# RG-LRU gate products as two 64-row matmuls on the halves of TensorE's array

## The chip, the cores and the metric

The kernel runs on one core of a Trainium2 chip. The metric is device time in microseconds of one execution. The engines are TensorE (PE, with its weight loads PEld), VectorE (DVE), ScalarE (ACT), GpSimd (POOL, nearly unused here) and SyncE (SP, which issues the transfers). One execution was profiled; the spans and rows below are from it.

## The reference, cut to what matters

One residual block of a streaming encoder on 512 tokens of width 1024: a Mamba-2 branch and an RG-LRU branch side by side, a gated merge of both, and a convolutional feed-forward part. The RG-LRU branch is what the change touches:

```python
gate = gelu(u_y)
xc = causal_dwconv(u_x, conv_w, conv_b)                  # 4 taps
xb = xc.reshape(b, s, 16, 64)                            # 16 blocks of 64 channels
r = sigmoid(einsum("bshi,hij->bshj", xb, wr) + br)       # each block has its own 64 x 64
i = sigmoid(einsum("bshi,hij->bshj", xb, wi) + bi)
log_a = -8 * r * softplus(-lam)
a = exp(log_a)
bx = sqrt(-expm1(2 * log_a)) * i * xc
h = associative_scan(a, bx)                              # h_t = a_t h_(t-1) + bx_t
y_b = h * gate
```

All of it is float32.

## The kernel before

Activations lie channel-major: 128 channels on the partitions, 512 tokens along the columns. Every float32 operand of a product is split in two (a high part in the fast matmul format, and the rest), and each product is three matmuls, high by high, high by low and low by high, that add up in one PSUM bank (`mm3`).

The weights come as 149 slabs of 128 x 1024. SyncE loads a slab (`raw`), ScalarE writes its high part (`whi`, L50 as all calls that keep their order) and VectorE its low part (`wlo`, L180). A slab is split two products ahead (`AHEAD = 2`). A product against the 1024-deep activations is 24 matmuls.

The order of TensorE's and of ScalarE's instructions is that of the code. VectorE's is put together by the compiler's planner from the code's order and its own costs. Work that follows a product is registered with `after(n, ...)` and written n slabs later, in `tick`; `step` holds back pieces of the Mamba-2 branch that fill VectorE between products.

The RG-LRU part runs over eight tiles of 128 channels, each with two of the 64-channel blocks. Tile i has its product, its convolution (`conv`, L225), two slabs later the split of `xc` and of the gate weights `wg` (`lru_split`, L611 and L612), and three slabs after its own product the gate products and what follows (`lru_gates`). So the gate group of tile i stands on TensorE behind the product of tile i + 2, and on ScalarE behind the first convolution step (`tmp<-ps,pcs`) of that product. The gate weights of a tile are two 128 x 128 matrices, one for r and one for i, each with two 64 x 64 blocks on its diagonal and zeros elsewhere. Each is one `mm3` and one tanh (sigmoid by tanh) with a bias per channel.

ScalarE then does an exp, a tanh (both `L<-tmp,nsp`) and a square; VectorE a multiplication with `xc` (L629) and one for the root (L632). After every fourth tile come a square root of 2048 columns on ScalarE, a multiplication of 2048 columns (L636) and four scans (L642) on VectorE. The buffers named `L` are four; two sets of three are needed, so the second set waits for the scans of the first.

Behind that the eight products of the gelu branch follow: `lru_out` multiplies gelu (ScalarE) by the scan's result (L660) and splits it (`Y`, L197); the merge needs all eight.

Of the kernel before, what the change touches and what calls it, by code (L numbers as in the profile page):

```python
# [8 lines left out]
F32 = mybir.dt.float32  # L9
# [5 lines left out]
P = 128  # L15
D = 1024          # model width = SSM inner = LRU width
S = 512           # tokens
KT = D // P       # contraction tiles of a 1024-deep product
TT = S // P       # token tiles, also the SSD chunks
HEADS = 16  # L20
HD = 64
# [4 lines left out]

# columns of the per-channel parameter array
C_SCW, C_SCB = 0, 48
# [5 lines left out]
N_PC = 356  # L34
# columns of the row parameter array
R_POST, R_POST2, R_HEAD = 0, D, 2 * D
# [3 lines left out]
class InOrder:  # L40
    """An engine whose instructions keep the order in which they are written here."""

# [11 lines left out]
def block_kernel(ctx: ExitStack, tc, x, slabs, wgate, pc, rows, out):  # L54
# [37 lines left out]

# [1 line left out]
    xts = []  # L94
# [10 lines left out]

# [1 line left out]
    pending, steps = [], []  # L107
# [5 lines left out]
    def step(cost, fn, *args):  # L113
        """A step for the vector engine, of that many microseconds."""
        steps.append((cost, fn, args))

    def next_slab():
        """What follows needs the tensor engine to have gone on, or another engine's result."""
        steps.append(None)
# [19 lines left out]

# [1 line left out]
    n_slabs = slabs.shape[0]  # L141
# [57 lines left out]
    def split_scaled(hi, lo, src, w):  # L199
        """Split of src * w, w one value per partition."""  # L200
        A.mul(hi, src, w)
        V.scalar_tensor_tensor(out=lo, in0=src, scalar=w, in1=hi.bitcast(F32),
                               op0=ALU.mult, op1=ALU.subtract)
# [7 lines left out]
    def product(acts):  # L211
        """One 128-column slab against [1024, 512] activations: [128 columns, 512 tokens]."""
        w = slab()
        acc = ps()
        accumulate(acc, w, acts)
        return acc

    def conv(acc, w0, bias, taps):
        """Causal depthwise convolution along the tokens."""
        t = tmp()  # L220
        A.activation(t, acc, AF.Identity, bias=pcs[:, bias:bias + 1],
                     scale=pcs[:, w0 + taps - 1:w0 + taps])
        for d in range(1, taps):
            w = w0 + taps - 1 - d
            V.scalar_tensor_tensor(out=t[:, d:], in0=acc[:, :S - d], scalar=pcs[:, w:w + 1],  # L225
                                   in1=t[:, d:], op0=ALU.mult, op1=ALU.add)
        low_parts()
        return t
# [6 lines left out]
    def use_sqrt():  # L235
        """Has the scalar engine ready for square roots."""
        A.activation(tiny.tile([P, 1], F32, tag="ready", name="ready"), EPS1, AF.Sqrt)

    def sumsq(src, s=None, junk=None):
        """Sums of squares along the columns."""  # L240
        if s is None:
            s = tiny.tile([P, 1], F32, tag="ssq", name="ssq", bufs=16)
        if junk is None:
            junk = work.tile([P, S], F32, tag="junk", name="junk", bufs=1)
        A.activation(junk, src, AF.Square, accum_out=s)  # L245
        return s

    def inv_rms(parts, width, e):
        """(sum of parts / width + e) ** -0.5, as two factors; one part may be [128, n]."""
        n = parts[0].shape[1]  # L250

        def t(name):
            return tiny.tile([P, n], F32, tag=f"{name}{n}", name=name, bufs=4 if n == 1 else 1)

        for s in parts[:-1]:
            b = t("mean")
            A.activation(b, s, AF.Identity, scale=1.0 / width, bias=e)
            e = b
        r = t("root")
        A.activation(r, parts[-1], AF.Sqrt, scale=1.0 / width, bias=e)  # L260
        v = t("var")
        V.tensor_scalar(out=v, in0=parts[-1], scalar1=1.0 / width, scalar2=e,
                        op0=ALU.mult, op1=ALU.add)
        V.reciprocal(r, r)
        q = t("step")
        if n == 1:
            V.scalar_tensor_tensor(out=q, in0=r, scalar=v, in1=r, op0=ALU.mult, op1=ALU.mult)
        else:
            V.tensor_mul(q, r, r)
            V.tensor_mul(q, q, v)  # L270
        V.tensor_scalar(out=q, in0=q, scalar1=-0.5, scalar2=1.5, op0=ALU.mult, op1=ALU.add)
        return r, q
# [3 lines left out]

# [1 line left out]
    use_sqrt()  # L278
# [17 lines left out]

# [1 line left out]
    def causal(value, name):  # L298
        m = const.tile([P, P], F32, name=name)      # value where column >= row
        G.memset(m, value)  # L300
        G.affine_select(out=m, in_=m, compare_op=ALU.is_ge, fill=0.0, base=0,
                        pattern=[[1, P]], channel_multiplier=-1)
        return m
# [4 lines left out]
    G.memset(ones, 1.0)  # L308
    halfb = const.tile([P, 32], F32, name="halfb")  # halves of br, bi, gate_b
    V.tensor_scalar_mul(halfb, pcs[:, C_BR:C_BR + 32], 0.5)  # L310
    nsp4 = const.tile([P, 8], F32, name="nsp4")     # -4 softplus(-lambda)
    nega = const.tile([P, HEADS], F32, name="nega")

    def softplus(u, e):
        """max(u, 0) + log1p(e) with e = exp(-|u|), the logarithm by its atanh series."""
        n = u.shape[1]
# [15 lines left out]

# [1 line left out]
    def ssd_input(j, dst=None):  # L334
# [96 lines left out]
    for g in range(2):  # L431
        ssd_input(10 + g, Cc[:, g, :])
        tick()
# [1 line left out]
    xs = big.tile([P, TT, D], F32, tag="C", name="xs", bufs=2)  # L435
# [57 lines left out]
    def carry(c, g):  # L493
        """What earlier chunks bring to this one, and the state after it."""
        h0 = c * HEADS + 8 * g
# [69 lines left out]

# [1 line left out]
    for j in range(2):  # L567
# [16 lines left out]

# [1 line left out]
    for c in range(2):  # L586
# [19 lines left out]
    xcs = big16("Y", F32R).rearrange("p (i two) s -> p i two s", two=2)  # L606
    wgs = big16("Y", F32R).rearrange("p i (two w c) -> p i two w c", two=2, w=2)

# [5 lines left out]
    def lru_gates(i, xc):  # L614
# [3 lines left out]
        aa, uu, qq = grp["t"]  # L618
        gates = []
        for w in range(2):  # L620
            rp = ps()
            mm3(rp, wgs[:, i, 0, w], wgs[:, i, 1, w], xcs[:, i % 4, 0], xcs[:, i % 4, 1], True, True)
            s = tmp()
            A.activation(s, rp, AF.Tanh, bias=halfb[:, 8 * w + i:8 * w + i + 1], scale=0.5)
            gates.append(s)
        sp = nsp4[:, i:i + 1]
# [18 lines left out]
    for i in range(KT):  # L645
        wg = tiny.tile([P, 2, P], F32, tag="wg", name="wg", bufs=2)
        tc.keep_in_program_order(nc.sync.dma_start(out=wg, in_=wgate[i]))
# [19 lines left out]

# [1 line left out]
    m1 = []  # L669
# [23 lines left out]

# [1 line left out]
    def row_tile(r0):  # L695
# [4 lines left out]
    def norm_add(acts, n_slab, e, row, res, tail, lead, target, done):  # L700
        """target = res + RMSNorm(acts @ W) * row; token tile by token tile over the last slabs."""
        first = work.tile([P, TT, S], F32, tag="M", name="first", bufs=1)
# [114 lines left out]

# [1 line left out]
    early = []  # L819
# [51 lines left out]
def _layout(x, mix_pre_norm, mix_post_norm, w_in, ssm_conv_w, ssm_conv_b, ssm_dt_bias, ssm_a_log,  # L871
# [5 lines left out]
    def cols(w):  # L877
        """[1024, 128 n]: slab j holds [row in tile, row tile, column] of its 128 columns."""
        n = w.shape[1] // P
        return w.reshape(KT, P, n, P).transpose(2, 1, 0, 3).reshape(n, P, D)  # L880

    def rws(w):
        """[K, 1024]: per column half, slabs of two 128-row tiles by 512 columns."""
        n = w.shape[0] // (2 * P)
# [8 lines left out]
    up = cols(np.asarray(w_ffn_up)[0])  # L893
    dts = np.zeros((1, P, KT, 8, HEADS), np.float32)     # the dt columns twice, then zeros
    dts[0, :, :, :2] = dtw.reshape(KT, P, 1, HEADS).transpose(1, 0, 2, 3)
# [8 lines left out]
    ])  # L904
    wgate = np.zeros((8, P, 2, P), np.float32)
    for n, g in enumerate((lru_wr, lru_wi)):
        g = np.asarray(g)[0].reshape(8, 2, HD, HD)
        for e in range(2):
            s = slice(e * HD, (e + 1) * HD)
            wgate[:, s, n, s] = g[:, e]  # L910

    def chan(v, n):
        """[taps, 128 n] to [128, n, taps]."""
        v = np.asarray(v)[0].reshape(-1, n, P)
# [27 lines left out]
```

## Time and profile before

| what | value |
|---|---|
| three runs | 887.65, 887.66, 889.61 us; median 887.66 us |
| profiled execution, first to last instruction | 885.8 us |
| granted TensorE clock, mean | 0.999 |
| TensorE busy | 872.5 us (98%), 4050 matmuls |
| TensorE weight loads | 724.0 us (82%) |
| VectorE busy | 519.9 us (59%) |
| ScalarE busy | 392.8 us (44%) |

The time of an execution lies some 1.9 us over the span from its first to its last instruction. Matmuls are pipelined: the duration shown for one is longer than the distance to the next. Line numbers are those of the kernel before; L50 is the helper that records TensorE's and ScalarE's calls in order, so these are told apart by their tiles.

### The profile page before, as it was taken

How to read it: one execution, taken by the hardware profiler on the slowest of the kernel's cores; microseconds unless marked ns; L12 is line 12 of the kernel's file. 1: busy time of each engine (PE TensorE's matmuls, PEld its weight loads, DVE VectorE, ACT ScalarE, POOL GpSimd, SP SyncE). 2: the span in 40 equal slices, each digit the busy share in tenths (PEclk: the TensorE clock that was granted, in tenths of full speed). 3: DMA queues.
4: the chain of work that ended last, by engine and by line, in shares of the span. 5: the costliest groups of instructions: out<-in, count | busy, mean ns of one | idle time of the engine just before them, and what ended most of it. 6: DMA issues, size and time to landing. Idle time of an engine off the chain costs nothing.

```text
span 885.8 us, 10176 instructions
## 1 busy us (share of the span) xinstructions
PE 872.5 (98%) x4050; PEld 724.0 (82%) x4050; DVE 519.9 (59%) x732; ACT 392.8 (44%) x602; POOL 1.7 (0%) x14
## 2 busy tenths in 40 slices
PE   7999999999999999999999999999999999999996
PEld 6888887888878888888888988888888888888885
DVE  6777657987874554344467566666666666223225
ACT  6454535579584334222355444444444444213222
POOL 0000000000000000000000000000000000000000
PEclk9999999999999999999999999999999999999999
DMA  6332232222325332222370022222222222322212
GB/s 224 102 137 95 95 118 84 92 87 72 142 96 182 128 119 72 96 95 95 102 252 27 25 94 96 95 95 96 95 95 95 95 95 95 117 98 95 95 48 96
DMA packets 26192, 91.61 MB, mean 103 GB/s; under 512 B 3040, under 2 KB 4256, under 8 KB 25632
## 3 DMA queue, kind: packets, MB, share of 16 engines
q1 hardware_dynamic: 26144, 90.95, 30.1%
q8 instruction: 32, 0.52, 0.2%
q14 instruction: 16, 0.13, 0.0%
HBM read 88.81 MB, written 2.13 MB: 103 GB/s over the span
## 4 chain that ended last, share of the span: by engine, by line
PE 88%; DVE 5%; ACT 5%; issue 1%; DMA 1%; SPq 0%; DVEq 0%; ACTq 0%
PE ps L50 88%; ACT L L50 1%; DVE L L642 1%; DMA raw<-slabs 1%; DVE wlo L180 1%; ACT whi L50 1%; ACT tmp L50 1%; DVE tmp L660 0%; DVE L L636 0%; ACT L50 0%; ACT junk L245 0%; ACT M L50 0%; DVE Y L197 0%; ACT Y L50 0%; ACT junk L50 0%
## 5 line engine op out<-in xcount | busy, mean ns | idle before, releaser
L180 DVE TENSOR_TENSOR wlo<-raw,whi 128x1024 fp32r<-128x1024 f32 x139 | 169.7, 1222 | 140.5 <-ACT whi L50 137.9
L50 PE MATMUL ps<-C,whi 128*128 128x512 f32 x768 | 241.6, 389 | 0.0
L50 PE MATMUL ps<-H,whi 128*128 128x512 f32 x720 | 224.1, 394 | 1.5 <-DVE H L50 1.5
L50 ACT CAST whi<-raw 128x1024 fp32r<-128x1024 f32 x137 | 143.0, 1045 | 110.9 <-PE ps L50 105.6
L50 PEld LDWEIGHTS ps<-C,whi 128*128 128x128 f32 x768 | 144.1, 188 | 29.9
L225 DVE SCALAR_TENSOR_TENSOR tmp<-ps,pcs,tmp 128x511 f32<-128x511 f32 (+1 forms) x156 | 116.6, 748 | 80.4 <-ACT tmp L50 77.9
L50 PE MATMUL ps<-C,wlo 128*128 128x512 f32 x416 | 161.8, 389 | 0.0
L50 PEld LDWEIGHTS ps<-H,whi 128*128 128x128 f32 x720 | 134.1, 188 | 31.1 <-issue 2.4
L50 PE MATMUL ps<-H,wlo 128*128 128x512 f32 x352 | 137.5, 391 | 0.4 <-DVE wlo L180 0.3
L50 ACT ACTIVATE tmp<-ps,pcs 128x512 f32<-128x512 f32 x68 | 53.1, 780 | 128.2 <-PE ps L50 128.2
L50 PEld LDWEIGHTS ps<-C,wlo 128*128 128x128 f32 x416 | 78.1, 188 | 16.1
L50 PE MATMUL ps<-whi,H 128*128 128x512 f32 x256 | 81.4, 394 | 0.0
L50 PEld LDWEIGHTS ps<-H,wlo 128*128 128x128 f32 x352 | 66.1, 188 | 15.2 <-DVE wlo L180 1.2
L50 PE MATMUL ps<-whi,Y 128*128 128x512 f32 x192 | 59.6, 389 | 0.0
L50 PEld LDWEIGHTS ps<-whi,H 128*128 128x128 f32 x256 | 48.1, 188 | 10.3 <-issue 0.5
L50 PE MATMUL ps<-wlo,H 128*128 128x512 f32 x128 | 49.9, 389 | 0.0
L50 ACT CAST Y<-tmp 128x512 fp32r<-128x512 f32 x24 | 14.9, 621 | 66.9 <-DVE tmp L690 36.8
L50 ACT ACTIVATE tmp<-ps,halfb 128x512 f32<-128x512 f32 x32 | 21.5, 687 | 49.6 <-PE ps L50 49.6
L50 PEld LDWEIGHTS ps<-whi,Y 128*128 128x128 f32 x192 | 36.0, 188 | 7.5
L50 PE MATMUL ps<-Y,whi 128*128 128x512 f32 x128 | 40.5, 396 | 0.2 <-DVE Y L197 0.2
L50 PE MATMUL ps<-whi,L 128*128 128x512 f32 x128 | 39.7, 389 | 0.0
L50 PE MATMUL ps<-wlo,Y 128*128 128x512 f32 x96 | 37.3, 389 | 0.0
(167 smaller groups left out, 848.1 us busy)
## 6 DMA issues: line engine op xcount, KB each, us to landing
raw<-slabs SPq DMA_DIRECT2D x149, 512.0 KB, 3.2
quad<-x SPq DMA_DIRECT2D x8, 512.0 KB, 4.3
M<-acsD SPq DMA_DIRECT2D x4, 1024.0 KB, 4.6
out<-tmp SPq DMA_DIRECT2D x8, 256.0 KB, 2.1
wg<-wgate SPq DMA_DIRECT2D x8, 128.0 KB, 3.3
quad<-rows SPq DMA_DIRECT2D x2, 512.0 KB, 4.7
pcs<-pc SPq DMA_DIRECT2D x1, 178.0 KB, 7.1
acsD<-acsT SPq DMA_DIRECT2D x1, 32.0 KB, 2.9
```

What stands on the lines that cost most here:

```text
L50: return lambda *args, **kw: self.tc.keep_in_program_order(op(*args, **kw))
L180: V.tensor_sub(*late.pop(0))
L225: V.scalar_tensor_tensor(out=t[:, d:], in0=acc[:, :S - d], scalar=pcs[:, w:w + 1], in1=t[:, d:], op0=ALU.mult, op1=ALU.add)
L642: V.tensor_tensor_scan(out=qq[:, e, :], data0=aa[:, e, :], data1=uu[:, e, :], initial=0.0, op0=ALU.mult, op1=ALU.add)
```

## The change

The zero blocks go. The gate weights of a tile become one 128 x 128 array: its upper 64 rows hold the r and i columns of the first block side by side, its lower 64 rows the i and r columns of the second. `wg` is loaded and split with half the columns. In place of two times three matmuls of 128 rows there are three pairs of 64-row matmuls; one of a pair works on the upper 64 partitions and the other on the lower, each into a PSUM bank of its own, `rps[0]` and `rps[1]`. Each bank then holds r in one half of its partitions and i in the other. The two tanh of 128 partitions become four of 64 partitions, all of 512 columns, two of which read one half of the partitions and write the other. Both banks and both `tmp` buffers are taken at the group's start. Comments were dropped from the file too.

```diff
-    wgs = big16("Y", F32R).rearrange("p i (two w c) -> p i two w c", two=2, w=2)
+    wgs = big16("Y", F32R).rearrange("p i (two w c) -> p i two w c", two=2, w=2)[:, :, :, 0, :]
...
-        gates = []
+        halves = slice(0, HD), slice(HD, P)
+        rps = ps(), ps()
+        for n, (u, v) in enumerate(((0, 0), (0, 1), (1, 0))):
+            for b in range(2):
+                mm(rps[b], wgs[halves[b], i, u], xcs[halves[b], i % 4, v], n == 0, n == 2)
+        gates = [tmp(), tmp()]
         for w in range(2):
-            rp = ps()
-            mm3(rp, wgs[:, i, 0, w], wgs[:, i, 1, w], xcs[:, i % 4, 0], xcs[:, i % 4, 1], True, True)
-            s = tmp()
-            A.activation(s, rp, AF.Tanh, bias=halfb[:, 8 * w + i:8 * w + i + 1], scale=0.5)
-            gates.append(s)
+            for b in range(2):
+                A.activation(gates[w][halves[b], :], rps[b][halves[w ^ b], :], AF.Tanh,
+                             bias=halfb[halves[b], 8 * w + i:8 * w + i + 1], scale=0.5)
...
-        wg = tiny.tile([P, 2, P], F32, tag="wg", name="wg", bufs=2)
+        wg = tiny.tile([P, P], F32, tag="wg", name="wg", bufs=2)
...
-    wgate = np.zeros((8, P, 2, P), np.float32)
-    for n, g in enumerate((lru_wr, lru_wi)):
-        g = np.asarray(g)[0].reshape(8, 2, HD, HD)
-        for e in range(2):
-            s = slice(e * HD, (e + 1) * HD)
-            wgate[:, s, n, s] = g[:, e]
+    wr, wi = (np.asarray(g)[0].reshape(8, 2, HD, HD) for g in (lru_wr, lru_wi))
+    wgate = np.concatenate([np.concatenate([wr[:, 0], wi[:, 0]], 2),
+                            np.concatenate([wi[:, 1], wr[:, 1]], 2)], 1)
```

## Rows read from the trace of the kernel before

**Rows 1.** The page, busy time of each engine, share of the span.

```profile
PE 872.5 (98%) x4050; PEld 724.0 (82%) x4050; DVE 519.9 (59%) x732; ACT 392.8 (44%) x602; POOL 1.7 (0%) x14
```

**Rows 2.** Stretches: length, PE, PEld, DVE, ACT, POOL busy us; clock, DMA share, GB/s.

```profile
155.00:184.00 29.00, 29.00 (x138) 24.28 (x137) 26.28 (x45) 18.00 (x25) 0.00 (x0) 1.00 0.29 94
...
200.00:220.00 20.00, 20.00 (x89) 16.48 (x89) 15.02 (x22) 19.63 (x25) 0.00 (x0) 1.00 0.25 79
220.00:232.00 12.00, 11.63 (x60) 9.35 (x59) 12.00 (x16) 4.50 (x7) 0.00 (x0) 1.00 0.36 133
...
260.00:880.00 620.00, 618.90 (x2878) 516.76 (x2878) 321.75 (x433) 240.03 (x368) 0.00 (x0) 1.00 0.29 100
```

**Rows 3.** The chain that ended last, 130 to 270 us: start us, us, what.

```profile
129.78 54.36 PE ps L50 x240
...
184.16 0.69 ACT tmp L50
...
190.18 1.65 DVE L L636
...
196.70 3.38 DVE L L642 x3
...
200.09 0.82 ACT L L50
...
218.03 2.29 DVE L L636
...
259.90 10.18 PE ps L50 x48
```

**Rows 4.** Waits from 155 to 260 us: in total, times, longest.

```profile
ACT L L50 <- DVE L L642: 5.1, 1, 5.1
...
PEld ps L50 <- DVE wlo L180: 1.2, 2, 0.8
```

**Rows 5.** TensorE's timeline, the gate group of tile 3: start us, us.

```profile
182.60 1.52 PE L50 MATMUL ps<-Y 128*128 128x512 f32 x6
```

**Rows 6.** Timeline around the 32-row transposes, matmuls (PE) and weight loads (PEld).

```profile
29.64 0.39 PE L50 MATMUL ps<-H,wlo 128*128 128x512 f32 x1
29.96 0.43 PE L50 MATMUL ps<-ident,tmp 32*128 32x32 f32 x4
30.32 0.72 PE L50 MATMUL ps<-H,whi 128*128 128x512 f32 x2
...
30.32 0.30 PEld L50 LDWEIGHTS ps<-H,whi 128*128 128x128 f32 x2
```

**Rows 7.** ScalarE's timeline, tanh and exp of tiles 3 and 5.

```profile
183.48 1.37 ACT L50 ACTIVATE tmp<-ps,halfb 128x512 f32<-128x512 f32 x2
184.75 1.51 ACT L50 ACTIVATE L<-tmp,nsp 128x512 f32<-128x512 f32 x2
...
203.09 1.25 ACT L50 ACTIVATE tmp<-ps,halfb 128x512 f32<-128x512 f32 x2
204.23 1.52 ACT L50 ACTIVATE L<-tmp,nsp 128x512 f32<-128x512 f32 x2
```

**Rows 8.** VectorE's timeline at 24 us, a copy of 32 lanes.

```profile
24.62 0.68 DVE L360 COPY tmp<-ps 32x512 f32<-32x512 f32 x1 [0.49 <-PE ps L50]
```

**Rows 9.** The tile `wg`: duration ns min/median/max, first and last start us.

```profile
L612 DVE TENSOR_TENSOR Y<-wg,Y x8: 414/419/426, 147.1 to 202.3; 128x256 fp32r<-128x256 f32 x8
```

**Rows 10.** VectorE's timeline, 208 to 225 us.

```profile
208.55 0.69 DVE L629 SCALAR_TENSOR_TENSOR L<-tmp 128x512 f32<-128x512 f32 x1
209.16 0.69 DVE L612 TENSOR_TENSOR Y<-tmp,Y 128x512 fp32r<-128x512 f32 x1
...
223.68 1.22 DVE L180 TENSOR_TENSOR wlo<-raw,whi 128x1024 fp32r<-128x1024 f32 x1
```

**Rows 11.** TensorE at tile 7's gate group, and its weight load at 225 us.

```profile
209.80 1.56 PE L50 MATMUL ps<-Y 128*128 128x512 f32 x6
...
224.95 0.19 PEld L50 LDWEIGHTS ps<-H,wlo 128*128 128x128 f32 x1 [0.45 <-DVE wlo L180]
```

## The prediction

> **What bounds the kernel now.** I began with the busy shares of the page: TensorE is busy for 98% of the span [rows 1]. That says that most of the time is a row of matmuls with hardly a gap, but not that every matmul taken out gives its time back. So the second view is the table of stretches around the change [rows 2]. From 260 us on TensorE waits for next to nothing. In 200 to 220 us, where the last gate products lie, ScalarE is busy 19.63 of 20 us, and in 220 to 232 us VectorE is busy all 12 us. Two other engines are full just there. The third view is the chain that ended last [rows 3]: one unbroken piece of TensorE up to 184.13 us, then ScalarE and VectorE alone until 259.90 us, then TensorE again. The reader is to see that for 76 us the end is set by the recurrence work that follows the gate products, while TensorE keeps itself busy from weights split in advance. The fourth view says how much TensorE has to spare there [rows 4]: its weight loads do wait for `wlo`, the low halves of the weights, though only 1.2 us in all. Its reserve is used up. Whatever makes the chain between 184 and 260 us later makes TensorE later by as much; whatever makes TensorE faster inside it turns into waiting.
>
> **TensorE's part.** One group of gate products is six matmuls in 1.52 us, the last of them 0.39 [rows 5]: they start 0.227 us apart, 1.36 us a group, 10.9 us for eight. Their number does not change. With two 64-row matmuls at a time in the two halves of the array, six take three slots, 0.68 us. Nothing in the trace runs two at a time, so concurrency itself is unseen; what can be checked is the weight load: two loads of 128 columns in a row take 0.30 us, one of them 0.19, so they lie 0.11 us apart [rows 6], so two fit a slot of 0.227 us. The change of shape is seen once, around the four 32-row transposes [rows 6]: the first starts 0.32 us after the full matmul ahead of it instead of 0.227, and behind them the first full matmul holds its successor off by 0.33 us (0.72 less the 0.39 of one). That is 0.1 us at each end; the last transpose ends some 0.08 us before the full matmul starts. I take 0.28 us for in and out. So one group is 0.68 + 0.28 = 0.96 us and gives 0.40 us, eight give 3.2 us. Bounds for the gain g of a group: 0.49 us if the 0.08 us is the transposes' own, 0.30 us if the second half starts a load (0.11 us) late; and -0.28 us if the halves run one after the other.
>
> The Trainium skill speaks of the same place: "TensorEngine Tiling (Array Packing)", Overview, gives a theoretical speedup of up to 2x for a dimension of 64, and its Tiling Modes says that changing the mode drains the engine. By the 2x alone g would be 0.68 us and the sum below +2.4 us; by the row with the change of shape it is +3.2 us. I go by the row; the trace agrees with the drain, 0.1 us at each end. The same page's PSUM Bottleneck says that tiling does not speed up the emptying of PSUM, which is here the tanh on ScalarE; 19.63 busy us of 20 [rows 2] bear that out for the stage behind tile 4.
>
> **ScalarE's part.** The two tanh (`tmp<-ps,halfb`, 128x512) become four of 64x512. The engine now needs 1.27 us from the first tanh of group 3 to the exp behind it (183.48 to 184.75), because the second half of the products comes 0.68 us after the first; where both are there in time it is 1.14 us (203.09 to 204.23), 0.57 us each [rows 7]. What half the lanes cost is not in the trace on this engine. The nearest row is VectorE's: a copy of 32 lanes by 512 columns takes 0.68 us [rows 8], an operation of 128 lanes by 512 columns 0.69 [rows 10]. The tanh keep their columns and lose only lanes, so I take 0.57 us for each half, 2.28 us for four; the lower bound is half of that, 0.29 us, with which four cost what two cost now. The extra is 2.28 - 1.27 = +1.0 us for group 3 and 2.28 - 1.14 = +1.14 us for those that run packed.
>
> The Trainium skill's "ScalarE: Activation LUTs", What ACT_TABLE_LOAD costs, counts one element per cycle in each lane, by which idle lanes save nothing and the sum is the +3.2 us below; no run here shows it for this engine.
>
> **The rest of the change.** VectorE splits 128 columns of `wg` in place of 256: the longer of its two operations is 0.42 us now [rows 9]. Halving the columns is worth at most 0.21 us for it and as much for the other. They end by 203 us and none lies on the chain, since in the part of it that is VectorE's the rows are others [rows 3]; so I count nothing; if one did lie on it, that would be a gain of at most 0.4 us. The eight loads of `wg` halve, and nothing on the chain waits for one. Both PSUM tiles are taken at once instead of in turn; two were in use before too. The arithmetic on the sums is the same. Costed at nothing, together.
>
> **The sum along the chain.** Each group k is worked off on ScalarE behind the convolution of the product ahead of it, so it moves with TensorE.
> 1. Where the chain leaves TensorE (group 3, 182.60 us), groups 0 to 2 have given 3 x 0.40: -1.2 us. ScalarE keeps up there: 18.0 us busy in the 29 us up to 184 [rows 2] with the work of three groups; with 1.0 more for each it is 21 in some 28.
> 2. Group 3's tanh: +1.0. The square root, the 2048-column multiplication and the four scans [rows 3] begin 0.2 us earlier.
> 3. Group 4's tanh lie ahead of the 5.05 us in which ScalarE waits for the scans to free a buffer [rows 4]: its 1.14 us vanish there.
> 4. Groups 5, 6 and 7 run on ScalarE without a pause up to the second square root: 3 x 1.14 = +3.4 us. At 218.03 us the chain is at -1.2 + 1.0 + 3.4 = +3.2 us.
> 5. From there VectorE is full to 232 us, and the `wlo` for which TensorE waits at 224.95 us [rows 10, 11] comes 3.2 us later, and so does TensorE. The rest of the chain and everything behind 259.90 us move along.
>
> TensorE meanwhile comes 3.2 us too early, so its waits grow by 6.4 us: some 2 us at the product behind group 6; up to 3 us at group 7, since the split of its input ends at 209.85 us, 0.05 us behind the group's start, and stands on VectorE behind the multiplication of 208.55 us that needs group 6's tanh [rows 10, 11]; and some 2 us at 225 us. The profiled execution has a span of 885.8 us; the median of the runs is 887.66, so 1.9 us lie around the span. I forecast 887.7 + 3.2 = **890.9 us**, slower by 0.36%. With g from 0.30 to 0.49 the sum is +3.5 to +2.9: 890.6 to 891.2, and with half a microsecond for the order on VectorE 890.3 to 891.6.
>
> **Rivals.**
> *The halves don't overlap.* For it: the trace has no pair that runs together. Against it: nothing but different rows, different banks and loads that fit. Then g is -0.28: +0.8 + 1.0 + 3.4 = +5.3 us, 893.0.
>
> *VectorE's order changes, and it is not slower.* VectorE's instructions are put in order by a planner, which will see other lengths. The multiplication of 190.18 us takes 2.29 us, as its twin at 218.03, and ends at 192.4; three scans take 3.38 us, so four directly behind it would end at 196.9 us in place of 200.0 [rows 3], and what VectorE does between them now, convolution and a weight split, would come later. ScalarE then goes on 3.1 us earlier, and the sum is +0.1, 887.8 us. It decides from a lead of 0.5 us on (3.2 less 2.7). For it: ScalarE's 5.05 us of waiting [rows 4] are just that order. Against it: the convolution was planned ahead of the scans, and no input of either changes places.
>
> *Half a tanh costs half.* With 0.29 us each, steps 2 and 4 fall away: -1.2 us, 886.5 us, since the chain still starts behind only three faster groups. Against it stands the copy of 32 lanes.
>
> *The gain arrives.* Cheap halves and scans first together would leave TensorE as the bound: -3.2 us, and at best the 1.2 us of waits that it has now [rows 4]: 883.3 to 884.5 us.
>
> *The clock.* The granted clock is 1.00 in each of the stretches [rows 2], and no wait there is longer than half a microsecond. Waits of 2 to 3 us close together are not in this stage of the trace. If the clock fell to the lower of its two levels behind one, half a product (12 slots of 0.227 us) would cost 2.7 us more: 893.6 us.
>
> **How the numbers follow.** A measurement of this kernel can tell about 0.3%, 2.7 us, from no change. Chances: the forecast 0.48; no overlap 0.13; clock 0.05; VectorE's order, wholly or in part (887.8 to 890.3), 0.21; cheap halves 0.05; the gain arrives 0.08. Slower by over 0.3%: 0.48 but for a small part, 0.13 and 0.05, so 0.63; within: 0.29; faster: 0.08. The range leaves out the gain that arrives and the far end of the worst cases: 886.4 to 893.6 us.
>
> **What the profile after would show.** Right: a group of gate products in about 1 us, with pairs that start together; four tanh in 2.3 us; ScalarE without a pause from about 200 to 221 us; TensorE waiting some 6 us in all between 200 and 235 us for `wlo` and for the input of group 7; nothing new behind 263 us. Wrong: groups of 1.6 us (no overlap); tanh of 0.3 us; scans that end before 198 us; granted clock under 1.00. A TensorE that reaches the last stage earlier than now would refute the reading that the chain, not TensorE, sets this stage.

## The result, and the profile after

Slower, and by twice the forecast: 7.1 us where 3.2 were forecast. The kernel after the change takes 896.17 us (median of 5 runs, 894.80 to 896.33), the kernel before 889.08 us beside it (5 runs): ratio 1.0081, 95% interval 1.0070 to 1.0092. Forecast was 890.9 us, with a range up to 893.6.

Runs of either kernel fall into two groups some 1.3 to 2 us apart, and the two profiled executions are of different ones: the four 32-row transposes start at 29.96 us before [rows 6] and at 31.24 us after, ahead of all that was changed. So times of the two traces are compared below after taking off 1.28 us, and spans are counted from the transposes on: 885.8 - 29.96 = 855.84 us before, 894.6 - 31.24 = 863.36 us after, +7.5 us.

The stretches of [rows 2], after (length, busy us of PE, PEld, DVE, ACT, POOL; clock, DMA share, GB/s):

```profile
155.00:184.00 29.00, 29.00 (x143) 22.30 (x141) 25.89 (x45) 21.52 (x30) 0.00 (x0) 1.00 0.24 83
200.00:220.00 20.00, 18.76 (x77) 13.73 (x76) 14.46 (x22) 17.18 (x25) 0.00 (x0) 0.91 0.18 61
220.00:232.00 12.00, 8.07 (x45) 6.54 (x43) 7.95 (x8) 9.25 (x10) 0.00 (x0) 0.94 0.30 118
260.00:880.00 620.00, 619.64 (x2884) 517.41 (x2883) 319.53 (x421) 243.51 (x365) 0.00 (x0) 1.00 0.28 98
```

TensorE, which before stood still for 0.4 us in the first three of these together, now does so for 1.2 us in the second and 3.9 in the third, and the granted clock, 1.00 before, falls in both. From 260 us on nothing is new. TensorE loses its time between 200 and 260 us.

TensorE's gate groups of tiles 1 and 2 and the matmul behind them, to be read beside [rows 5], and its waits:

```profile
170.13 0.96 PE L50 MATMUL ps<-Y 64*128 64x512 f32 x6
176.69 0.97 PE L50 MATMUL ps<-Y 64*128 64x512 f32 x6
177.58 0.73 PE L50 MATMUL ps<-H,whi 128*128 128x512 f32 x2
...
203.99 0.73 PE L50 MATMUL ps<-Y 64*128 64x512 f32 x4 [0.52 <-DVE Y L612]
204.92 0.73 PE L50 MATMUL ps<-H,whi 128*128 128x512 f32 x2 [0.20 <-ACT whi L50]
206.18 0.50 PE L50 MATMUL ps<-H,wlo 128*128 128x512 f32 x1 [0.52 <-DVE wlo L180]
...
229.95 0.78 PE L50 MATMUL ps<-H,whi 128*128 128x512 f32 x2 [2.66 <-ACT whi L50]
232.32 0.79 PE L50 MATMUL ps<-H,wlo 128*128 128x512 f32 x1 [1.59 <-DVE wlo L180]
```

The pairs run together: the two matmuls of a pair start within 0.01 us, the three pairs of the second group at 176.69, 177.02 and 177.26 us, and six take 0.97 us, the last of them 0.39. A tile takes 176.69 - 170.13 = 6.56 us, where before it took 6.80 (groups of tiles 2 and 3 at 175.80 and 182.60 us). So TensorE has its gain, 0.24 us a group. Its two waits behind 226 us are for one slab, number 33 counted from 0, which the fifth product of the gelu branch reads: first for its high part, then for its low part.

ScalarE's timeline, to be read beside [rows 7]:

```profile
184.25 2.82 ACT L50 ACTIVATE tmp<-ps,halfb 64x512 f32<-64x512 f32 x4
187.09 1.52 ACT L50 ACTIVATE L<-tmp,nsp 128x512 f32<-128x512 f32 x2
...
217.15 2.79 ACT L50 ACTIVATE tmp<-ps,halfb 64x512 f32<-64x512 f32 x4
219.96 1.52 ACT L50 ACTIVATE L<-tmp,nsp 128x512 f32<-128x512 f32 x2
221.51 0.63 ACT L50 ACTIVATE tmp<-L 128x512 f32<-128x512 f32 x1
```

From the first of four half tanh to the exp behind them 2.84 us pass (2.81 in the later groups), where with two full ones it was 1.27 or 1.14. The chain that ended last (start us, us, what) leaves TensorE earlier than before, and shows how:

```profile
129.89 34.69 PE ps L50 x160
164.58 0.67 ACT tmp L50
...
184.96 0.69 ACT tmp L50
185.64 0.03 issue
185.67 0.69 ACT tmp L50
...
202.45 0.82 ACT L L50
...
225.40 2.29 DVE L L641
...
231.13 1.14 DVE wlo L180
232.28 0.04 issue
232.32 37.95 PE ps L50 x149
```

One tanh of 0.69 us, 0.03 us of nothing, the next: they start 0.71 us apart, where two full ones of 0.69 us started 0.57 us apart. The second multiplication of 2048 columns, L636 at 218.03 us in [rows 3], is now L641 at 225.40 us: 6.1 us later without the 1.28. TensorE's wait for the low part of slab 33 moves from 224.95 us [rows 11] to 232.32 us, also 6.1 us later. The clock does the rest (columns as above):

```profile
226.00:232.00 6.00, 2.07 (x14) 1.39 (x12) 6.00 (x6) 3.33 (x5) 0.00 (x0) 0.87 0.43 175
232.00:238.00 6.00, 5.68 (x15) 4.49 (x16) 6.00 (x9) 2.06 (x3) 0.00 (x0) 0.56 0.25 89
238.00:244.00 6.00, 6.00 (x28) 4.96 (x27) 4.53 (x6) 3.56 (x8) 0.00 (x0) 1.00 0.26 87
```

Behind the two waits (2.66 and 1.59 us) TensorE runs at 0.56 of its clock, near the lower of its two levels (1.2 of 2.4 GHz): matmuls 0.427 us apart in place of 0.227. The 24 matmuls from the low part at 232.32 us on take 7.9 us, as against 6.1 us before from 224.95 us on, where the last wait of the stage lay among them:

```profile
231.05 0.50 PE L50 MATMUL ps<-H,wlo 128*128 128x512 f32 x1 [0.35 <-DVE wlo L180]
```

### The profile page after: what moved, and what is told of

It reads as the page before. It is cut to its first block, busy times and chain, and to the rows that moved or that the text cites. A ratio compares the mean times of both kernels' runs of the same rounds, so it can differ in the third digit from the quotient of the medians.

```text
span 894.6 us, 10199 instructions
## 1 busy us (share of the span) xinstructions
PE 875.8 (98%) x4050; PEld 721.9 (81%) x4050; DVE 519.5 (58%) x732; ACT 404.5 (45%) x618; POOL 1.7 (0%) x14
## 4 chain that ended last, share of the span: by engine, by line
PE 89%; ACT 6%; DVE 3%; DMA 1%; issue 1%; SPq 0%; DVEq 0%; ACTq 0%
PE ps L50 89%; ACT tmp L50 3%; ACT L L50 2%; DMA raw<-slabs 1%; DVE L L647 1%; ACT whi L50 1%; DVE L L641 0%; ACT junk L245 0%; ACT L50 0%; DVE wlo L180 0%; DVE tmp L225 0%; DVE tmp L737 0%; SPq L97 0%; DVE tmp L275 0%; DVE quad L746 0%
## 5 line engine op out<-in xcount | busy, mean ns | idle before, releaser
L50 PE MATMUL ps<-H,whi 128*128 128x512 f32 x720 | 229.3, 402 | 4.5 <-ACT whi L50 2.9
L50 PEld LDWEIGHTS ps<-H,whi 128*128 128x128 f32 x720 | 136.1, 192 | 37.7 <-issue 4.2
L50 PE MATMUL ps<-H,wlo 128*128 128x512 f32 x352 | 139.8, 397 | 2.1 <-DVE wlo L180 2.1
L50 ACT ACTIVATE tmp<-ps,halfb 64x512 f32<-64x512 f32 (+1 forms) x48 | 32.9, 685 | 51.2 <-PE ps L50 50.5
```

Source lines behind the costliest of these rows:

```text
L50: return lambda *args, **kw: self.tc.keep_in_program_order(op(*args, **kw))
```

## The experiments

Each kernel's ratio is to the kernel before, run beside it. The last column is the span from the transposes on, less the 855.84 us of before, of one traced execution each. e4 had one run, with strips behind its end, and is not in the table.

| kernel | median us | ratio, 95% interval | later by, us |
|---|---|---|---|
| after the change | 896.17 | 1.0081 [1.0070, 1.0092] | 7.5 |
| e1, pairs, full tanh | 888.68 | 0.9995 [0.9986, 1.0005] | -0.3 |
| e2, before, half tanh | 895.22 | 1.0080 [1.0063, 1.0097] | 6.9 |
| e3, before, four full tanh | 893.51 | 1.0057 [1.0042, 1.0073] | 5.6 |
| e5, other order of halves | 894.85 | 1.0081 [1.0066, 1.0096] | 7.3 |
| e6, fill for the clock | 893.80 | 1.0066 [1.0054, 1.0079] | 6.3 |
| e7, relief by VectorE | 895.25 | 1.0088 [1.0074, 1.0102] | 7.8 |
| e8, the same on before | 893.32 | 1.0054 [1.0039, 1.0068] | 4.1 |
| e9, two slabs by GpSimd | 892.82 | 1.0052 [1.0038, 1.0065] | 5.1 |
| e10, e1 with two slabs by GpSimd | 887.16 | 0.9993 [0.9984, 1.0001] | -0.3 |
| e11, before with two slabs by GpSimd | 887.24 | 0.9990 [0.9981, 0.9999] | -0.8 |
| e12, three slabs by GpSimd | 889.95 | 1.0029 [1.0019, 1.0038] | 2.6 |

Behind the stage of the change the traces still drift apart, by up to 0.7 us. Read at the first matmul of the merge that takes the branch's result (`ps<-Y,whi`, 254.26 us before and 263.30 us after), the loss is 7.8 us after the change, 7.6 in e2 and e5, 6.2 in e3, 6.1 in e6, 5.7 in e9 and 2.6 in e12; e1, e10 and e11 lie within 0.4 us of before.

**One part alone.** e1 keeps the pairs and drops the half tanh, which leaves r and i exchanged for half of the channels; e2 keeps the half tanh and drops the pairs.

```diff
 e1 (on after)
-            for b in range(2):
-                A.activation(gates[w][halves[b], :], rps[b][halves[w ^ b], :], AF.Tanh, ...)
+            A.activation(gates[w], rps[w], AF.Tanh, bias=halfb[:, 8 * w + i:8 * w + i + 1], scale=0.5)
 e2 (on before)
-            A.activation(s, rp, AF.Tanh, bias=halfb[:, 8 * w + i:8 * w + i + 1], scale=0.5)
+            for h in (slice(0, HD), slice(HD, P)):
+                A.activation(s[h, :], rp[h, :], AF.Tanh, bias=halfb[h, ...], scale=0.5)
```

> The changed kernel with two tanh of all 128 lanes per gate group in place of four of 64; it leaves out putting r and i back in their places, so the gates of half the channels are exchanged. Theory A (ScalarE's four half tanh, start to start 0.71 us, cause the loss): a group costs ScalarE 1.14 us again, the chain at the second multiplication of 2048 columns is about 0.5 us ahead of before, no wait of TensorE over 1 us, clock 1.00; 0.5 to 1.5 us faster than before. Rival B (TensorE's pairs, with their change of shape, and the clock cause it): the loss stays at over 3 us. Rival C (VectorE's new order causes it): about 3 us slower, the scans ending as late as in the changed kernel.

> The kernel before with its full matmuls, and only each of its two tanh cut in two of 64 lanes. Theory A: four take 2.82 us; +1.5 us at group 3 and 3 x 1.7 at groups 5 to 7 make the chain some 6.5 us later, and a lower clock behind the wait adds up to 2 us: 6.5 to 8.5 us slower than before. Rival B: ScalarE has room for them and the loss is under 2 us.

The half tanh by themselves make the whole loss; the pairs by themselves cost nothing and bring nothing that can be told from nothing (-0.3 us of the trace, an interval of about 0.9 us to either side), less than the 0.5 to 1.5 us expected: between 205 and 233 us TensorE waits 1.5 us at four places, at a clock of 1.00. In e2 four half tanh take 2.78 us, TensorE waits longer still for slab 33, and the clock falls to 0.63 (226 to 232 us):

```profile
229.01 1.22 PE L50 MATMUL ps<-H,whi 128*128 128x512 f32 x2 [4.00 <-ACT whi L50]
231.38 0.80 PE L50 MATMUL ps<-H,wlo 128*128 128x512 f32 x1 [1.15 <-DVE wlo L180]
```

Half tanh without faster products are late by the same chain.

**What about the half tanh is dear: their number or their halves?** e3 runs each full tanh of the kernel before twice, the second time into a tile that nothing reads.

```diff
+            A.activation(work.tile([P, S], F32, tag="junk", name="junk", bufs=1), rp, AF.Tanh,
+                         bias=halfb[:, 8 * w + i:8 * w + i + 1], scale=0.5)
```

> The kernel before with each gate tanh done twice on all 128 lanes, the second into a scratch tile that nothing reads. As many instructions as with the halves. If operations of half the lanes are slower in a row than full ones (theory A's mis-sized term), four take 2.28 us here, the chain is some 4.4 us later, and the time is 4 to 6 us longer than before, 2 to 3 us less than with the halves. Rival: four tanh cost 2.8 us whatever their lanes, and the time is that of the halves.

ScalarE's timeline, the first two of four:

```profile
183.60 0.69 ACT L50 ACTIVATE tmp<-ps,halfb 128x512 f32<-128x512 f32 x1
184.18 0.68 ACT L50 ACTIVATE junk<-ps,halfb 128x512 f32<-128x512 f32 x1
```

Four full tanh start 0.57 us apart, and the kernel loses some 1.2 us less by the trace than with four halves (5.6 as against 6.9; at the merge 6.2 and 7.6), not 2 to 3 us less as expected; the intervals of the ratios overlap. So most of the loss is the doubled number, and a part is a property of the halves. e4 looks for that property: the kernel before, with strips of eight bare tanh behind its end (and with 64-row matmuls, once on both halves in turn and once on one half).

```diff
...
+    strip("s_full", [(al, al)])
+    strip("s_low", [(lo, lo)])
+    strip("s_turn", [(lo, lo), (hi, hi)])
+    strip("s_cross", [(lo, lo), (hi, hi), (lo, hi), (hi, lo)])
+    strip("s_wide", [(slice(0, 96), slice(0, 96))])
...
```

> The kernel before with strips of bare operations behind its end; the block itself is complete. Eight tanh of 512 columns from PSUM in a row: 128 lanes 0.57 us start to start. If fewer lanes cost the overlap, 64 lanes take 0.71 us in all three arrangements (same half, halves in turn, halves crossed) and 96 lanes too. Rival: only a turn from one half to the other costs it; then the same half takes 0.57 us. If half the lanes cost half, 0.29 us. Then 24 matmuls of 64 rows on alternating halves: 12 slots of 0.227 us, 2.7 us, if they overlap; 5.4 us if not, and 5.4 us for 24 on one half alone.

ScalarE's timeline:

```profile
883.05 4.74 ACT L50 ACTIVATE s_full<-ps,halfb 128x512 f32<-128x512 f32 x8
887.63 4.71 ACT L50 ACTIVATE s_low<-ps,halfb 64x512 f32<-64x512 f32 x8
892.19 5.60 ACT L50 ACTIVATE s_turn<-ps,halfb 64x512 f32<-64x512 f32 x8
897.82 5.56 ACT L50 ACTIVATE s_cross<-ps,halfb 64x512 f32<-64x512 f32 x8
903.39 4.71 ACT L50 ACTIVATE s_wide<-ps,halfb 96x512 f32<-96x512 f32 x8
```

128, 96 and 64 lanes cost the same, 0.57 us from one start to the next, so long as all eight work on the same partitions. Each strip takes its two PSUM banks in turn, so the change of bank is not the cause. Where the half changes from one to the next, it is 0.70. The number of lanes has no part in it; the turn has. TensorE's strips show the pairs again: on the halves in turn the matmuls start two by two, 0.427 us from pair to pair while the clock is at its lower level, and 24 take 5.13 us at a mean clock of 0.63 (2.7 us were expected, at the full clock); on one half they start one by one, 0.227 us apart, and 23 take 5.50 us at 1.00. e5 then orders the four half tanh by the half that they write, so that it turns once instead of three times.

```diff
-        for w in range(2):
-            for b in range(2):
+        for b in range(2):
+            for w in range(2):
```

> The changed kernel with the four half tanh in the order low, low, high, high of the partitions that they write; nothing is left out. Theory (a turn from one half to the other costs the overlap, as the strips show; 0.70 instead of 0.57 us): four take 2.4 us instead of 2.8, the chain at the second multiplication of 2048 columns is 4 x 0.4 = 1.6 us earlier, 1 to 2.5 us less than the changed kernel, so 4.5 to 6 us slower than before. Rival (a turn of the half that is read counts as well): four take 2.7 us and at most 0.5 us comes back.

No gain, as its rival had it: the four still take 2.79 us. From one tanh to the next only one thing turns now, first the half that is read, then the one that is written, then again the one that is read. A turn of either costs the overlap.

**The clock.** e6 gives TensorE 20 matmuls that nothing reads, ahead of the fifth product of the gelu branch, where after the change it waits.

```diff
+        if i == 4:
+            idle = ps()
+            for _ in range(20):
+                mm(idle, hT[0][:, 0, 0:P], hT[0][:, 1, :])
```

> The changed kernel with 20 matmuls of 128 rows by 512 columns into a bank that nothing reads, put where TensorE waits some 3 us ahead of the fifth product of the gelu branch; the block is complete. Theory (the lower clock behind that wait costs 1.8 us of its own): the clock stays at 1.00 from 226 to 240 us, 24 matmuls behind the wait take 5.5 us instead of 7.9, and the time is 1 to 2 us less than the changed kernel's. Rival (the chain alone sets the time there): no difference, or up to 1.5 us longer for the extra work.

TensorE's timeline and the stretches of e6:

```profile
225.48 4.79 PE L50 MATMUL ps<-H 128*128 128x512 f32 x20
230.11 0.61 PE L50 MATMUL ps<-H,whi 128*128 128x512 f32 x2
230.76 0.50 PE L50 MATMUL ps<-H,wlo 128*128 128x512 f32 x1
```

```profile
226.00:232.00 6.00, 5.97 (x26) 4.62 (x25) 6.00 (x8) 2.06 (x3) 0.00 (x0) 1.00 0.54 187
232.00:238.00 6.00, 5.63 (x25) 4.34 (x24) 6.00 (x9) 2.62 (x5) 0.00 (x0) 1.00 0.27 85
```

With the wait filled the clock stays at 1.00, and 24 matmuls take 6.1 us, a wait of 0.37 us among them. Useless work made the kernel 1.2 us faster by the trace than after the change (6.3 as against 7.5; at the merge 6.1 and 7.8), and 0.15% by the ratios, whose intervals overlap.

**Relief of ScalarE.** e7 (order of e5) and e8 (the kernel before) let VectorE write the high parts of slabs 30 to 33, and send one tanh of tile 4 to a `tmp` buffer, so that ScalarE need not wait for the scans there.

```diff
+    ON_DVE = (30, 31, 32, 33)
...
-            A.copy(hi, raw)
+            if i in ON_DVE:
+                V.tensor_copy(hi, raw)
+            else:
+                A.copy(hi, raw)
...
-        A.activation(qq[:, e, :], gates[0], AF.Tanh, bias=sp, scale=sp)
+        th = tmp() if i == 4 else qq[:, e, :]
+        A.activation(th, gates[0], AF.Tanh, bias=sp, scale=sp)
...
```

> The order low, low, high, high, and ScalarE relieved in that stage: the high parts of four weight slabs (30 to 33) are written by VectorE, and the tanh of tile 4 goes to a tile of its own, so that ScalarE doesn't wait for the scans; the block is complete. Theory (ScalarE's share of the chain is the whole loss): 1.6 + 3.4 + 3 x 1.04 = 8.1 us off a chain that is 6.1 us late; TensorE sets the time again, with eight groups 0.24 us shorter and most of its waits gone: 1 to 3 us faster than before. Rival (VectorE, full from 220 to 232 us and now with four casts more, takes its place): within 1.5 us of before.

> The kernel before with the same relief and its own matmuls and tanh; the block is complete. Theory: the chain gets some 8 us of room that TensorE, already busy, can't use; only its waits of some 1.5 us there go, so 0 to 1.5 us faster than before, and 1 to 2 us slower than with the pairs. Rival: the relief by itself explains what the version with pairs gains, and both are equal.

Both failed in the same way. VectorE's order changed, and the split of the convolution's result of tile 6 came late. TensorE in e8:

```profile
207.75 0.49 PE L50 MATMUL ps<-Y 128*128 128x512 f32 x1 [2.79 <-DVE Y L615]
208.95 1.57 PE L50 MATMUL ps<-Y 128*128 128x512 f32 x5 [0.71 <-DVE Y L616]
```

In e7 the same waits are 4.80 and 1.45 us. They say nothing of ScalarE's part; whether VectorE has room for the high parts in another order stays open.

**The way by which the loss reaches TensorE.** GpSimd is idle in this stage. e9 (on after), e10 (on e1) and e11 (on before) let it write the high parts of slabs 32 and 33, e12 (on after) those of 32 to 34. The chain through tanh, multiplication and scans keeps its instructions; the splits no longer stand in ScalarE's queue, which by itself makes the second multiplication 0.9 us earlier than after the change (slab 32 was split ahead of the last tanh).

```diff
-            A.copy(hi, raw)
+            (G.tensor_copy if i in (32, 33) else A.copy)(hi, raw)
```

> The kernel after the change, but GpSimd, which is idle, writes the high parts of the weight slabs 32 and 33 in place of ScalarE, so that neither the split of these two slabs nor TensorE waits for ScalarE's long row of half tanh any more. The order on VectorE changes only in that the two low parts come earlier. Theory: in the kernel after, the loss reaches TensorE through these two slabs alone (waits of 2.66 and 1.59 us behind 226 us). They vanish, but slab 34 is still split behind ScalarE's cast that needs the scans (235.13 us), so TensorE then waits for it some 3 to 4 us, from 233 us on, and reaches the end of that product 2.0 to 3.6 us earlier than after: 892.5 to 894.0 beside 896.2. Rival 1: the whole wait moves to slab 34, gain under 1 us. Rival 2: GpSimd's copy of 128 x 1024 takes so long, or holds VectorE up so much, that the low parts come as late as now: no gain or a loss.

> As the first of these four, with slab 34 on GpSimd too. Theory: the wait for slab 34 goes, slab 35 is the next that stands behind the casts which need the scans (its high part at 240.9 us in the kernel after, where TensorE would now be ready at 239 us): 3 to 4.5 us faster than after, so 891.7 to 893.2 beside 896.2, and at least as fast as with two slabs. Rival: VectorE, full there, makes the low part of slab 34 ahead of the 2048-column multiplication and so delays the scans by 1.2 us: no more gain than with two slabs, or less.

> Pairs of 64-row matmuls, two tanh of all lanes (the gates of half of the channels are exchanged), and the high parts of slabs 32 and 33 on GpSimd. Theory: the two tanh leave the chain where it was before the change, TensorE has at most some 2 us of waits to give back around 203 to 232 us; 0.5 to 1.5 us below the same kernel without GpSimd (888.7 beside 889.0 of before), so 887 to 888.2 where before is at 889: a version that beats both, by 0.1 to 0.2%. Rival: pairs and relief give nothing, because the scans set the rest: the same as before within 0.3 us.

> The kernel before, with the high parts of slabs 32 and 33 on GpSimd. Theory: at most the wait of 0.45 us for the low part at 224.95 us and its neighbour go (1.2 us in all); gain 0 to 1.2 us. Rival: TensorE's spare time is used up, so a change of VectorE's order costs it as it did when VectorE itself wrote the high parts (+5.7 us); here VectorE has no more work than before, so no loss is expected by the theory.

TensorE in e9, then in e12 its last wait of the stage and the stretches behind it:

```profile
233.62 0.73 PE L50 MATMUL ps<-H,whi 128*128 128x512 f32 x2 [1.38 <-ACT whi L50]
235.29 0.50 PE L50 MATMUL ps<-H,wlo 128*128 128x512 f32 x1 [0.94 <-DVE wlo L180]
```

```profile
205.43 0.80 PE L50 MATMUL ps<-H,wlo 128*128 128x512 f32 x1 [1.25 <-DVE wlo L180]
```

```profile
202.00:208.00 6.00, 4.04 (x12) 2.69 (x13) 5.93 (x9) 5.90 (x9) 1.49 (x1) 0.73 0.25 87
208.00:214.00 6.00, 6.00 (x21) 4.49 (x22) 4.19 (x6) 5.87 (x9) 0.59 (x1) 0.70 0.29 90
```

e9 came out as the theory had it: the wait moves to slab 34, shorter (2.3 us where 3 to 4 were expected), and 2.4 us of the 7.5 are gone. In e12 TensorE waits for nothing behind 206 us and 4.9 us are gone, somewhat more than expected; slab 35 is no wait. Yet in e12 the second L641 multiplication still starts 5.2 us later than before (223.00 us with the transposes at 29.77; 218.03 and 29.96 before). So the late scans as such cost TensorE little: they cost it through the weight splits that stand behind them in the queues of ScalarE and VectorE. What is left in e12, 2.6 us, is around 204 us: waits of 0.52, 0.20 and 1.25 us, and a clock that then falls to 0.73 and 0.70. As an estimate from rows: the mean clock of those 12 us puts some 6.8 us of them at the lower level, which at 0.427 for 0.227 us a matmul costs 3.2 us; with the waits, 2.0 in place of 0.5 us, and less 8 x 0.24 us for the pairs that is +2.8 us. It is no more than an estimate: behind the same waits e9's clock was 0.80 and 0.92.

e10 brought nothing over e1, as its rival had it, but not because of the scans: TensorE waits for the split of `xc` (1.1 us) and for a low part (1.3 us), more together than the eight pairs save (1.9 us), and both came late because of the help. GpSimd and VectorE in e10, then in e11:

```profile
209.81 1.09 POOL L171 CAST whi<-raw 128x1024 fp32r<-128x1024 f32 x1 [7.06 <-PE ps L50]
209.92 1.52 DVE L612 TENSOR_TENSOR Y<-tmp,Y 128x512 fp32r<-128x512 f32 x1
```

```profile
209.73 1.61 POOL L171 CAST whi<-raw 128x1024 fp32r<-128x1024 f32 x1 [4.55 <-PE ps L50]
210.36 2.06 DVE L180 TENSOR_TENSOR wlo<-raw,whi 128x1024 fp32r<-128x1024 f32 x1
```

Beside GpSimd's copy the split of `xc` took 1.52 us for 0.69, the low part 2.06 us for 1.22. In e9, e10 and e12 another operation, ahead of the low part that TensorE awaits around 205 us, took 1.52 or 1.53 us for 0.68, and that wait is 1.25 us where it is 0.52 after the change and 0.31 in e1. So a part of what is left in e12 is a price of the help, and what the pairs would gain with a helper that does not hold VectorE up, no run here shows.

e11 is the fastest kernel of the study that leaves no part of the computation out or changed, 0.1% below before with an interval that just leaves out 1; its trace is 0.8 us shorter (0.3 us at the merge), and TensorE's waits for `wlo` are gone, as expected (0 to 1.2 us).

## Why the prediction was half right

The sign, the place and the mechanism held. The chain between 184 and 260 us set the end; TensorE's gain inside it turned into waiting; half the lanes saved nothing; group 4's extra vanished in the wait for the scans (5.1 us [rows 4], now 3.4). The step that failed in the sum is that of ScalarE's part, "I take 0.57 us for each half, 2.28 us for four". The chain at the second multiplication was to be 3.2 us late and was 6.1:

- *Half tanh: +2.2 us more.* They lie 0.71 us apart, not 0.57: four take 2.82 us. The 0.57 us is the distance between two full tanh; the row for one alone has 0.69. The overlap of neighbours was carried over to instructions that turn between partition halves, and there it is gone (e4, e5). From the first tanh to the exp, group 3: 2.84 - 1.27 = +1.6 in place of +1.0; groups 5 to 7: 3 x (2.81 - 1.14) = +5.0 in place of +3.4.
- *Pairs: +0.5 us more.* g is 0.24, not 0.40, below its bound of 0.30. The overlap was costed rightly (a pair in one slot, 0.23 us), the change of shape was not: from the last full matmul ahead (176.37 us) to the third one behind (178.16 us) 1.79 us pass, 1.11 more than three full ones take, so going in and out costs 0.43 us and not 0.28. The prediction counted the first matmul's hold on its successor on the way out alone; the first pair holds off the second as well (0.33 us from 176.69 to 177.02). Three groups ahead of the chain gave 0.7 us and not 1.2.
- *The start of group 3: +0.2 us.* Its first pair stands 0.32 us behind the full matmul ahead of it in place of 0.227, and its first tanh 1.00 us behind that in place of 0.88. The chain now goes over to ScalarE at group 0 and not at group 3, but that adds nothing to the sum: up to group 3 ScalarE starts its convolution steps 6.56 us apart (177.00 and 183.56 us), which is TensorE's own pace.

*The clock* was a rival of its own, with a chance of 0.05 and a price of 2.7 us. It came on top of the forecast: the waits that the prediction itself had worked out (some 2, up to 3 and some 2 us) are of the kind that it called absent from the trace, and it did not ask what the clock does behind them. Its sentence that no wait there is longer than half a microsecond holds for the matmuls alone: a weight load waited 0.8 us [rows 4]. The price was 1.8 us by the product that ran slow, and by e6 1.7 us at the merge, 1.2 us over the whole span. There is a first fall at 202 to 214 us, whose cost ends in TensorE's later wait.

So: +3.2 forecast, +2.2 and +0.5 for the two terms, +0.2 for the start of group 3, +1.8 for the clock, 7.9 us. At the merge 7.8 are measured, over the whole span 7.5; a wait of 0.2 us for Y at 259.90 us before, which is gone, is a part of the difference, and the rest stays open.

Of what was to be seen after: groups of about 1 us, right (0.97); pairs together, right; four tanh in 2.3 us, wrong (2.8); ScalarE without a pause from 202 to 227 us, right; some 6 us of TensorE's waits, right (5.5) but placed otherwise: 1.2 us at group 6 and the product behind it, none at group 7, and most behind 226 us, first for `whi`, which stands on ScalarE behind the tanh; clock of 1.00, wrong. Scans first, cheap halves and the gain that arrives did not happen: the first scans ended 1.1 us later than before (202.43 and 200.06 us), not 3 us earlier.

The Trainium skill's "ScalarE: Activation LUTs", What ACT_TABLE_LOAD costs, has one element per cycle in each lane, and e4's strips of 128 and of 64 lanes agree (4.74 and 4.71 us). The same section says that ACTIVATEs in a row overlap by some 93 ns. The strips come near it for equal partitions (0.69 us long, 0.57 apart, 0.12 us) and not for halves in turn, where the overlap is nil.

## What to carry to other kernels

Cost what a faster product does to the work that empties its banks: splitting a full-lane instruction in two halves doubles it, and where the halves take turns it also loses the overlap of neighbours, so a layout that leaves the next engine its full lanes is worth more than the rows saved. When a prediction turns a gain into waits of two microseconds and more on TensorE, price the granted clock behind them in the same sum. And look at what else stands in the queue of the late engine: two or three splits taken out of ScalarE's queue gave back a third to two thirds of a loss whose cause stayed in place. But price the helper too: beside GpSimd's copies single VectorE operations took 0.8 us longer, and TensorE waited for them.

## What the runs showed of the hardware

- ScalarE overlaps neighbouring tanh of 512 columns by 0.12 us, with 128, 96 or 64 lanes alike. If the half of the partitions that is read or written changes from one to the next, it does not: 0.70 us from start to start for 0.57.
- Two 64-row matmuls on the two halves of TensorE start together, and the next pair 0.23 us later; the change of shape into and out of six of them costs 0.43 us.
- The clock fell to 0.56 over 6 us behind waits of 2.66 and 1.59 us, and to 0.73 and 0.70 behind waits of 0.52, 0.20 and 1.25 us (0.80 and 0.92 in another run with the same waits). In e10 single waits of 1.25 and 1.10 us, some 7 us apart, left it at 1.00.
- GpSimd's copy of 128 x 1024 to the fast matmul format took 1.0 to 2.2 us, where ScalarE takes 1.04. Beside it single VectorE operations took 1.52 us for 0.68 and 2.06 us for 1.22; beside the longest copy (2.19 us, e11) they kept nearly their usual lengths.
